# Ten of stage two's twelve units by seven block products, 13.6 filler products a run, and the third row pair's blocks loaded earlier in the queue

## The chip, the cores and the metric

The kernel runs on one core of one Trainium2 chip. The metric is the device time of one execution in microseconds (us), the median of the runs taken. Engines are named as in the profile: PE is TensorE's matmul, PEld its weight load, DVE is VectorE, ACT is ScalarE, POOL is GpSimd, SP is the engine that issues most transfers.

## What is computed

One layer (DEPTH is 1, so only mixer A runs) of an encoder over 2048 tokens of width 1024, 16 heads of 64, all in float32: a root-mean-square norm, one projection to queries, keys, values and a gate, 2-D neighbourhood attention on a 32 x 64 grid of tokens (8 x 16 neighbours, with a learned bias), a SiLU gate, the output projection, the residual and a last norm. Cut to what matters:

```python
h = rmsnorm(x, norm_0)
q, k, v, gate = split(h @ w_in_0, 4)
# per token: softmax over its 8 x 16 neighbours of q.k / 8 + bias, then the weighted sum of v
o = neighbourhood_attention(q, k, v, rpb_0)
x = x + (o * silu(gate)) @ w_out_0
return rmsnorm(x, norm_f)
```

## The kernel before

Float32 products are made of three matmuls on "fp32r" halves: each operand is split into a high part h (a copy on ACT) and a low part l (a subtraction on DVE), and h·h, h·l and l·h are added in PSUM. Nearly every matmul of the projections moves 512 columns against a 128 x 128 weight.

The program has four stages, written out by hand in one order for all engines; each engine then works off its own part of that order and waits only for data and buffers.

- **Stage one** (tokens 0 to 1023) and **stage two** (tokens 1024 to 2047) make the projections. A unit is 256 columns of q, k, v or g. `seven_products` computes a unit for 1024 tokens as a 2 x 2 block product with seven block products in place of eight (84 matmuls in place of 96); the sums of weight blocks (`sum_`), the splits (`form`) and the sums of results (`add`, `out_`) are extra work on DVE and ACT. In stage two `units_two` lists the units done so; before, nine of twelve: k, q and g of column groups 0, 1 and 2.
- **The attention stage** is a loop over m, 33 passes ("runs"). Run m makes the scores of one pair of heads and one tile of 512 tokens (`scores`: PE L1297; minimum and bias on DVE L1306; exponentials on ACT L1312), turns the weights of the pair before (`turns`: PE transposes `ph`, L1355; copies to `pta` on ACT L1345 and DVE L1343) and multiplies them with the values (`values`: PE `o`, L1374; the gate on DVE L1378). The order in it is: filler products, transposes of m-1, scores of m, values of m-1. Between the scores of m and their transposes lies one stretch of filler in run m+1: in it DVE takes a reciprocal of the sums (L1317), and POOL (L1324) and DVE (L1322) scale the weights (`normalise`). `feed(8)` puts eight filler products, with whatever copies, gates and splits fall due in them, ahead of that reciprocal in DVE's order; the rest of the filler comes behind it.
- **The filler** is, first, the projections that stage two left over (`projections`, plain products, 24 matmuls a group, PE L392 to L396; `halves` lists them; each group ends in `give`: for q and k a copy on ACT, for g a tanh on ACT L372 and a product on DVE L373), and then the output products of token tiles 0 to 5 (`outputs`, PE L1578 to L1582, 24 matmuls a group; each group ends in `add_rows`, a sum on DVE L1450). `split_og` splits a tile of the gated attention output into `gh` (ACT L1420) and `gl` (DVE L1421). `dense` is the number of filler products a run, and `amount` the list by run (alternately 1.5 more and less from run 8 to 23).
- **The last stage**, `rows_by_seven`, makes the output products of tiles 6 to 15 in five pairs, again seven block products a pair (PE `py`, L1670). `load_rows_of` (L1631) loads a block of a pair from the scratch `ogd`; `sum_rows` (L1643) adds blocks on DVE; `land` (L1602) brings the split blocks of the output weights. All of these transfers are issued by SP, in order. Buffers come from pools: `raw` has six, `qp` (the queries' pool) two.

Queries, keys, values and gates pass through scratch memory; each run loads those of the next.

Of the kernel before, what the change touches and what calls it, by code (L numbers as in the profile page):

```python
# [77 lines left out]
def build(ctx, tc, x, xr, xt, wg, bias, w_out, n0, nf, out):  # L78
# [22 lines left out]
    qp = pool("qp", 2)  # L101
# [155 lines left out]
    def units(k, j):  # L257
        return [KINDS[k] + j + i for i in range(2 if k == "v" else 1)]

    units_two = [(k, j) for j in range(3) for k in "kqg"]  # L260
    halves = [(k, 3, 1, c) for g in ("k", "qg") for c in (2, 3) for k in g]
    attending = [False]
    last_use = {}
    for n, (k, j, ph, c) in enumerate(halves):
# [5 lines left out]
    for n, (k, j, ph, c) in enumerate(halves):  # L270
        a = (KINDS[k] + j, ph)
# [66 lines left out]
    def store(key, lag, f):  # L338
        n = len(later)
        while n and later[n - 1][0] > clock[0] + lag:  # L340
            n -= 1
        later.insert(n, (clock[0] + lag, key, f))
# [853 lines left out]
    def projections():  # L1196
        for n, (kind, j, ph, c) in enumerate(halves):
            state["half"] = n
            w = (KINDS[kind] + j, ph)
            for a in range(2):  # L1200
                if n == len(halves) - 5 and a == 0:
                    for k in range(RES_EARLY):
                        load_res(*turns_[k])
                if n == len(halves) - 1:
                    if a == 0:
                        load_og(0)
                        load_og(1)
                    else:
                        store(("og0",), 9, lambda: split_og(0))
                consume(1)  # L1210
                p = yield from group(w, a, c, n)
                state["event"] = clock[0]
                give(kind, 2 * j + a, c, p, True)
            state["done_halves"] = n + 1
# [199 lines left out]
    def split_og(n):  # L1414
        t = G[n]
        state["event"] = clock[0]
        h, l = wp([128, NK, 128], F32R, "gh"), wp([128, NK, 128], F32R, "gl")
        for j in range(2):
            s = slice(4 * j, 4 * j + 4)
            nc.scalar.activation(h[:, s], t[:, s], AF.Copy)  # L1420
            nc.vector.tensor_tensor(l[:, s], t[:, s], h[:, s].bitcast(F32), OP.subtract)  # L1421
        G[n] = [(h[:, i], l[:, i]) for i in range(NK)]
# [176 lines left out]
    def land(where, homes):  # L1599
        for (f, k, i), h in zip(where, homes):  # L1600
            TF.setdefault(f, [[None, None] for _ in range(4)])[k][i] = h
            nc.sync.dma_start(h.bitcast(F32), wod[f][:, k, i])  # L1602
# [13 lines left out]
    def land_T2():  # L1616
        for f in ("A21", "A22"):
            load_rows_of(1, f, vh)
        for m in range(LEADERS):
            load_rest_of(m)  # L1620
        land([("T2", k, i) for k in range(4) for i in range(2)], [a[k, 1] for k in range(4) for a in (woh, wol)])

    def land_T4():
        land(parts7[17:], sixths() + [sp([128, 512], F32R, "t")])

    def load_rows_of(m, f, home=None):
        n, half = PAIRS[m][int(f[1]) - 1], int(f[2]) - 1
        T, i = divmod(n, 4)
        must(*[("og", p, T) for p in range(NP) if slot(T, p) // 4 == half])
        A[m, f] = (home or raw)([128, 512], F32, "raw")  # L1630
        nc.sync.dma_start(A[m, f].rearrange("p (k q) -> p k q", k=4), ogd[T][:, i, 4 * half:4 * half + 4])  # L1631
# [65 lines left out]
    def rows_by_seven():  # L1697
# [10 lines left out]
        def on(i, f, *a):  # L1708
            todo.setdefault(i, []).append((f, a))
# [4 lines left out]
            on(i, sum_rows, 1, f)  # L1714
        for i, f in ((8, "S1"), (9, "S2"), (10, "S3"), (12, "S4")):
            on(i, sum_rows, 2, f)
        for i, f in ((2, "A21"), (4, "A22")):
            on(i, load_rows_of, 2, f)
        for m in range(E, len(PAIRS)):
            s = seq.index((m, 6)) - 1  # L1720
            for d, f in ((-12, "A11"), (-10, "A21"), (-9, "A22"), (-7, "A12")) if m == E else \
# [18 lines left out]
                        f(*a)  # L1740

    cycles = len(order)
    dense, end_of_it = 16.5, 24
    amount = [dense] * 25
    first = 16
    amount[0] -= first / 2
# [56 lines left out]
    for m in range(cycles + 1):  # L1803
        a = amount[m] - 8
# [88 lines left out]
```

## Time and profile before

| what | us |
|---|---|
| median of 3 runs | 997.81 (997.7, 997.81, 1002.13) |
| the profiled execution, its own time | 1003.56 |
| its span, first to last instruction | 1001.5 |
| stage one, and the values of stage two, to about | 390 |
| stage two's nine units | 390 to 561 |
| attention stage | 561 to 895 |
| last stage | 895 to 1001.5 |

The span is 2 us shorter than the execution's own time. Rows of the timeline read: start, duration, engine, line and operation, count, and in brackets the idle time of the engine before the row and what ended it. Rows of the stretches read: the stretch, its length, busy time of PE, PEld, DVE, ACT and POOL with the number of instructions, the granted PE clock (1.00 is full), the share of the transfer engines, GB/s.

### The profile page before, as it was taken

The page shows a single profiled execution, that of the slowest core. Times are in us where ns is not written, and L with a number is a line of the kernel's source. Part 1 is how long each engine was busy: PE and PEld are TensorE (multiplying, and loading weights), DVE is VectorE, ACT ScalarE, POOL GpSimd, SP SyncE. Part 2 cuts the span into 40 slices and gives each one's busy share as a digit, 9 for nine tenths or more (in the row PEclk, how much of TensorE's full clock was granted, in tenths as well). Part 3 has the DMA queues.
Part 4 walks back from the last instruction along what each step waited for, and adds up shares of the span by engine and source line. Part 5 has one row for each costly group of instructions (what it writes and reads, how often), then busy time and mean ns, then how long its engine had stood idle before and what let it go on. Part 6 is the DMA issues. An engine that isn't in the chain of part 4 may idle for free.

```text
span 1001.5 us, 19560 instructions
## 1 busy us (share of the span) xinstructions
PE 991.0 (99%) x6904; PEld 793.1 (79%) x6904; DVE 772.4 (77%) x1704; ACT 520.4 (52%) x1271; POOL 149.5 (15%) x233
## 2 busy tenths in 40 slices
PE   9999999999999999999999999999999999999897
PEld 6888888888888888888888777777777777788786
DVE  5899888997666876766775677778888888885776
ACT  7873344454534433343434466667767666653443
POOL 0000001321100000000000123233333323212010
PEclk9999999999999999999999999999999999999999
DMA  8943547777957845655565798979887789799464
GB/s 288 340 128 96 196 142 252 240 245 256 348 162 224 259 134 182 220 185 184 200 205 179 220 281 244 277 239 287 286 252 255 207 263 286 243 335 319 132 187 116
DMA packets 149834, 227.67 MB, mean 227 GB/s; under 512 B 13608, under 2 KB 65064, under 8 KB 149736
## 3 DMA queue, kind: packets, MB, share of 16 engines
q1 hardware_dynamic: 147144, 222.09, 69.5%
q0 software_dynamic: 2160, 3.93, 2.4%
q8 instruction: 55, 0.90, 0.3%
q10 hardware_dynamic: 432, 0.40, 0.1%
q14 instruction: 43, 0.35, 0.1%
HBM read 160.31 MB, written 66.06 MB: 226 GB/s over the span
## 4 chain that ended last, share of the span: by engine, by line
PE 93%; DMA 4%; DVE 2%; ACT 1%; issue 0%; SPq 0%; DVEq 0%
PE pp L448 40%; PE pv L614 13%; PE o L1374 8%; PE s L1297 7%; PE py L1670 5%; PE ph L1355 4%; PE pp L394 2%; PE po L1578 2%; PE po L1580 2%; PE pp L396 2%; PE po L1582 2%; PE pp L392 2%; PE pv L729 2%; DMA raw<-ogd 1%; DMA ogd<-og 1%; DMA wol<-wodT 1%
## 5 line engine op out<-in xcount | busy, mean ns | idle before, releaser
L448 PE MATMUL pp<-h,f 128*128 128x512 f32 x576 | 185.4, 389 | 0.0
L1324 POOL TENSOR_SCALAR x<-x,st 128x360 f32<-128x360 f32 (+5 forms) x192 | 106.3, 570 | 521.5 <-DVE st L1317 520.2
L448 PE MATMUL pp<-t,f 128*128 128x512 f32 x702 | 171.6, 389 | 0.0
L448 PEld LDWEIGHTS pp<-t,f 128*128 128x128 f32 x702 | 131.6, 188 | 27.9 <-DVE u L461 0.4
L1312 ACT ACTIVATE x<-x,st 128x360 f32<-128x360 f32 (+5 forms) x256 | 134.1, 525 | 22.1 <-DVE st L1306 22.1
L448 PEld LDWEIGHTS pp<-h,f 128*128 128x128 f32 x576 | 108.1, 188 | 23.0 <-ACT p L456 0.5
L448 PE MATMUL pp<-l,f 128*128 128x512 f32 x288 | 112.1, 389 | 0.0
L1306 DVE CUSTOM_DVE_ANT_0 x<-s,em 128x360 f32<-128x360 f32 (+5 forms) x256 | 102.7, 456 | 3.6 <-PE s L1297 1.3
L431 DVE TENSOR_TENSOR f<-raw,f 128x512 fp32r<-128x512 f32 x105 | 75.9, 727 | 20.0 <-ACT f L430 19.8
L1374 PEld LDWEIGHTS o<-pta,vt 120*64 120x64 f32 (+2 forms) x1024 | 68.7, 137 | 22.4 <-DVE st L1306 15.2
L430 ACT ACTIVATE f<-raw 128x512 fp32r<-128x512 f32 x105 | 63.5, 622 | 38.6 <-DVE raw L437 22.0
L1374 PE MATMUL o<-pta,vt 120*64 120x192 f32 (+5 forms) x1024 | 83.5, 316 | 0.0
L1345 ACT ACTIVATE pta<-ph 120x512 f32<-120x512 f32 (+5 forms) x96 | 47.3, 557 | 59.4 <-PE ph L1355 59.4
L1343 DVE COPY pta<-ph 120x512 f32<-120x512 f32 (+5 forms) x96 | 56.1, 638 | 23.1 <-PE ph L1355 22.8
L1297 PE MATMUL s<-kt,q 64*64 64x360 f32 (+5 forms) x1024 | 71.3, 412 | 0.0
L448 PEld LDWEIGHTS pp<-l,f 128*128 128x128 f32 x288 | 54.1, 188 | 11.2
L614 PE MATMUL pv<-wh,t 128*128 128x512 f32 x176 | 56.2, 389 | 0.0
L1670 PE MATMUL py<-woh,f 128*128 128x512 f32 x160 | 52.2, 399 | 3.1 <-DVE y L1450 3.1
L448 PE MATMUL pp<-sixths,f 128*128 128x512 f32 x198 | 52.7, 389 | 0.0
L469 POOL TENSOR_TENSOR tmp<-tmp,rb 128x512 f32<-128x512 f32 x18 | 28.4, 1579 | 158.8 <-DVE tmp L466 128.0
L1297 PEld LDWEIGHTS s<-kt,q 64*64 64x64 f32 x1024 | 37.3, 132 | 18.6 <-ACT pta L1345 0.4
L1355 PEld LDWEIGHTS ph<-ident,x 64*120 64x120 f32 (+2 forms) x1408 | 42.5, 128 | 11.3 <-issue 9.2
(226 smaller groups left out, 1872.9 us busy)
## 6 DMA issues: line engine op xcount, KB each, us to landing
raw<-in_wg_dram SPq DMA_DIRECT2D x124, 256.0 KB, 5.0
row<-in_xr_dram SPq DMA_DIRECT2D x32, 256.0 KB, 5.2
vd<-v SPq DMA_DIRECT2D x32, 256.0 KB, 3.5
sgd<-sg SPq DMA_DIRECT2D x32, 256.0 KB, 5.1
q<-qd SPq DMA_DIRECT2D x32, 256.0 KB, 5.5
sgt<-sgd SPq DMA_DIRECT2D x32, 256.0 KB, 6.8
ogd<-og SPq DMA_DIRECT2D x32, 256.0 KB, 2.8
kt<-kd SPq DMA_DIRECT2D x16, 480.0 KB, 6.9
```

The lines of the kernel that those rows point to most:

```text
L430: nc.scalar.activation(t[:, 0], src, AF.Copy)
L431: nc.vector.tensor_tensor(t[:, 1], src, t[:, 0].bitcast(F32), OP.subtract)
L448: nc.tensor.matmul(B[n, P], t[:, int(m == 2), c], x[k][int(m == 1)], start=P in (1, 6, 5) and k == 0 and m == 0, stop=k == 3 and m == 2, s ...
L614: nc.tensor.matmul(p, a[:, o], b, start=P in (1, 6, 5) and k == 0 and m == 0, stop=k == 3 and m == 2, skip_group_check=True)
L1297: nc.tensor.matmul(places[C, s][h * 64:h * 64 + 64], qt[a, g * 64:g * 64 + 64], kt[a, :r1 - r0, c0:c0 + 8 * WIDE[C]].rearrange("p r (s c) ...
L1306: nc.vector.tensor_tensor_reduce(X[i, C][s], pst[s], EM[p, ROW_TYPE[T]][C > 0][s], -1.0, 1e38, OP.add, OP.min, st[:, o:o + 1])
L1312: nc.scalar.activation(X[i, C][s], X[i, C][s], AF.Exp, bias=st[:, o:o + 1], scale=-1.0, accum_out=st[:, 4 + o:5 + o])
L1324: nc.gpsimd.tensor_scalar(X[i, C][s], X[i, C][s], st[:, o:o + 1], 1.0, op0=OP.mult, op1=OP.mult)
L1343: nc.vector.tensor_copy(o, i_)
L1355: nc.tensor.transpose(ph[b, h][:k, o:o + 64], X[2 * m + late_, group[g]][s][q, at:at + k], ident[q, q])
L1374: nc.tensor.matmul(o[s * 64:s * 64 + 64, g0 * 64:g1 * 64], vt[:k, strip, s * 64:s * 64 + 64], t[:k, n * 64:(n + g1 - g0) * 64], start=stri ...
L1670: nc.tensor.matmul(B[m, P], t[:, a, c], b, start=P in (1, 6, 5) and k == 0 and i == 0, stop=k == 3 and i == 2, skip_group_check=True)
```

## The change

`units_two` gets a tenth unit, k of column group 3, and `halves` loses k's two halves: 84 matmuls come into stage two, and 96 leave the filler. `dense` goes from 16.5 to 13.6, so that the filler still lasts for all runs. The loads of the first residual block, of tiles 0 and 1 of the gated output, and the split of tile 0, which hang on positions in `halves`, are put at other positions. In the last stage the blocks A21 and A22 of the third pair (m = 2) are loaded at the end of `land_T2`, into the queries' pool, in place of at steps 2 and 4 of the sequence into `raw`.

```diff
-    units_two = [(k, j) for j in range(3) for k in "kqg"]
-    halves = [(k, 3, 1, c) for g in ("k", "qg") for c in (2, 3) for k in g]
+    units_two = [(k, j) for j in range(3) for k in "kqg"] + [("k", 3)]
+    halves = [(k, 3, 1, c) for c in (2, 3) for k in "qg"]
...
-                if n == len(halves) - 5 and a == 0:
+                if n == 0 and a == 1:
                     for k in range(RES_EARLY):
                         load_res(*turns_[k])
                 if n == len(halves) - 1:
-                    if a == 0:
+                    if a == 1:
                         load_og(0)
                         load_og(1)
-                    else:
-                        store(("og0",), 9, lambda: split_og(0))
+                        store(("og0",), 14, lambda: split_og(0))
...
         land([("T2", k, i) for k in range(4) for i in range(2)], [a[k, 1] for k in range(4) for a in (woh, wol)])
+        for f in ("A21", "A22"):
+            load_rows_of(2, f, qp)
...
-        for i, f in ((2, "A21"), (4, "A22")):
-            on(i, load_rows_of, 2, f)
...
-    dense, end_of_it = 16.5, 24
+    dense, end_of_it = 13.6, 24
```

The filler products that stand between two blocks of transposes on PE, counted in the order of the program (run m is the run in whose filler they stand):

| m | 2 | 3 | 4 | 5 | 11 | 12 | 13 | 17 | 19 | 21 | 26 | 27 | 28 |
|---|---|---|---|---|---|---|---|---|---|---|---|---|---|
| before | 18 | 15 | 16 | 17 | 15 | 21 | 12 | 15 | 15 | 15 | 16 | 17 | 19 |
| now | 10 | 14 | 13 | 14 | 12 | 16 | 12 | 12 | 12 | 9 | 13 | 13 | 13 |

Because the filler's groups now end at other places, other copies and splits fall ahead of the reciprocal. DVE in run 3, from the gate of the values (og) to the copies of the transposes, before:

```order
L1378 TENSOR_TENSOR og<-o,sgt 128x512
L1317 RECIPROCAL st<-st 128x4
L1322 TENSOR_SCALAR x_5999<-x_5999,st 128x264
L1322 TENSOR_SCALAR x_6000<-x_6000,st 128x264
L194 TENSOR_TENSOR w<-raw,w 128x512
L1343 COPY pta<-ph_6072 88x6x64
```

and now:

```order
L1377 TENSOR_TENSOR og<-o,sgt 128x512
L373 SCALAR_TENSOR_TENSOR sg<-sg,pp 128x512
L1316 RECIPROCAL st<-st 128x4
L1321 TENSOR_SCALAR x_5780<-x_5780,st 128x264
L1321 TENSOR_SCALAR x_5781<-x_5781,st 128x264
L542 SCALAR_TENSOR_TENSOR raw<-raw,g_174,rb 128x512
L547 TENSOR_TENSOR l<-raw,h 128x512
L1342 COPY pta<-ph_5852 88x6x64
```

A gate's product (sg) now stands ahead of the reciprocal, and a norm and a split of an input block (L542, L547) stand between the scaling and the copies. The filler group on which sg waits ends with the seventh product of this run.

DVE in run 26, before:

```order
L1378 TENSOR_TENSOR og<-o,sgt 128x512
L1450 TENSOR_TENSOR y<-po,xr 128x512
L1317 RECIPROCAL st<-st 128x4
L1322 TENSOR_SCALAR x_9702<-x_9702,st 128x288
L1322 TENSOR_SCALAR x_9703<-x_9703,st 128x288
L1492 SCALAR_TENSOR_TENSOR y<-y,st_8349,acc_175 128x512
L1492 SCALAR_TENSOR_TENSOR y<-y,st_8349,acc_176 128x512
L1421 TENSOR_TENSOR gl<-ograw,gh 128x512 x2
L1343 COPY pta<-ph_9780 96x6x64
```

and now:

```order
L1377 TENSOR_TENSOR og<-o,sgt 128x512
L1449 TENSOR_TENSOR y<-po,xr 128x512
L1420 TENSOR_TENSOR gl<-ograw,gh 128x512 x2
L1316 RECIPROCAL st<-st 128x4
L1321 TENSOR_SCALAR x_9750<-x_9750,st 128x288
L1321 TENSOR_SCALAR x_9751<-x_9751,st 128x288
L1420 TENSOR_TENSOR gl<-ograw,gh 128x512 x2
L1342 COPY pta<-ph_9830 96x6x64
```

The split of tile 4 has moved ahead of the reciprocal: the sixth filler product of this run is the first one that reads it, so it is made there and then. In the same way the split of tile 0 now stands ahead of the reciprocal in run 11.

SP at the start of the last stage, from the last of the T2 weights on, before:

```order
L1602 DMA wol<-wodT_95 128x512
L1602 DMA sixths<-wodT_97 128x512 x6
L1602 DMA t<-wodT_97 128x512
L1381 DMA ogd_88<-og 512x1x128
L1496 DMA out_dram<-y 128x512 x4
L1631 DMA raw<-ogd_87 128x512 x2
L1631 DMA raw<-ogd_88 128x512 x4
```

and now:

```order
L1601 DMA wol<-wodT_95 128x512
L1632 DMA raw<-ogd_87 128x512 x2
L1601 DMA sixths<-wodT_97 128x512 x6
L1601 DMA t<-wodT_97 128x512
L1380 DMA ogd_88<-og 512x1x128
L1495 DMA out_dram<-y 128x512 x2
L1632 DMA raw<-ogd_88 128x512 x4
```

The third pair's two blocks (from `ogd_87`) are now asked for ahead of the seven T4 weights, the last store of the attention output and the output rows.

## The prediction

> **What bounds the kernel now.** I read first the page's busy times and then what PE waited for.
>
> ```profile
> PE 991.0 (99%) x6904; PEld 793.1 (79%) x6904; DVE 772.4 (77%) x1704; ACT 520.4 (52%) x1271; POOL 149.5 (15%) x233
> PE py L1670 <- DVE y L1450: 3.1, 2, 2.8
> PE zp L135 <- DVE z L132: 1.2, 1, 1.2
> ```
>
> PE sets the end. In the whole span it waits in two places that count: at the start, and once in the last stage, 2.8 us on a sum of DVE. So a matmul saved is saved in full, if no new wait takes its place. The stretches show where one could:
>
> ```profile
> 390.00:561.00 171.00, 171.00 (x756) 141.65 (x755) 114.79 (x184) 62.83 (x112) 0.00 (x0) 1.00 0.61 198
> 658.00:893.00 235.00, 235.00 (x2855) 177.62 (x2853) 201.30 (x637) 160.07 (x493) 77.51 (x138) 1.00 0.85 264
> ```
>
> Stage two (first row) has DVE at 115 of 171 us, so another unit finds room there. In the attention stage (second row) DVE is busy 201 of 235 us, 86%, and PE is full only because the filler covers a chain of other engines. One run of that stage, from its block of transposes to the next one:
>
> ```profile
> 664.95 1.51 PE L1355 MATMUL ph<-ident,x 64*120 64x64 f32 x44
> 671.31 0.50 PE L394 MATMUL pp<-l,w 128*128 128x512 f32 x1
> 671.57 0.58 ACT L1312 ACTIVATE x<-x,st 128x360 f32<-128x360 f32 x1
> 672.28 0.18 DVE L1317 RECIPROCAL st<-st 128x4 f32<-128x4 f32 x1 [0.16 <-ACT x L1312]
> 672.62 1.34 POOL L1324 TENSOR_SCALAR x<-x,st 128x360 f32<-128x360 f32 x2 [0.32 <-DVE st L1317]
> 674.93 1.51 PE L1355 MATMUL ph<-ident,x 64*120 64x64 f32 x44
> ```
>
> This is run 11. The interval is 9.98 us with 15 filler products, which begin at 671.31. The chain runs over the last exponential (its accumulator is read by 672.2), the reciprocal and POOL's scaling, and is done at 673.96, 9.01 us after 664.95. PE came 0.97 us later, so it did not wait. Other runs have less to spare:
>
> ```profile
> 662.10 0.69 DVE L373 SCALAR_TENSOR_TENSOR sg<-sg,pp 128x512 f32<-128x512 f32 x1 [0.64 <-ACT sg L372]
> 662.70 0.17 DVE L1317 RECIPROCAL st<-st 128x4 f32<-128x4 f32 x1
> 663.07 1.83 POOL L1324 TENSOR_SCALAR x<-x,st 128x360 f32<-128x360 f32 x2 [1.42 <-DVE st L1317]
> 693.94 1.85 POOL L1324 TENSOR_SCALAR x<-x,st 128x360 f32<-128x360 f32 x2
> 695.73 1.51 PE L1355 MATMUL ph<-ident,x 64*120 64x64 f32 x44
> ```
>
> In run 10 a gate's product stands ahead of the reciprocal: the chain ends at 664.90, only 0.05 us before the transposes of 664.95. In run 13 (last two rows) POOL ended at 695.79, 0.06 us after the transposes had begun, and PE lost nothing: their first products read the weights scaled earlier. POOL's second piece is first read by the sixteenth of the 44 transposes; at 1.44 us for 44 that leaves 0.47 us of grace.
>
> **The matmuls.** 756 products took 171 us, 0.2262 each. 84 come, 96 go: 12 x 0.2262 = 2.7 us less. The tenth unit's sums and splits, 114.8 / 9 = 12.8 us of DVE in 19 us of PE, hide under its products; without that cover they would cost at most what exceeds 19 us, so nothing.
>
> **The third pair.** The one wait in the last stage:
>
> ```profile
> 906.50 4.30 SPq L1602 DMA_DIRECT2D sixths<-wodT  x6
> 916.02 0.41 SPq L1631 DMA_DIRECT2D raw<-ogd  x1
> 924.97 0.39 PE L1670 MATMUL py<-sixths,f 128*128 128x512 f32 x1
> 927.46 2.88 PE L1670 MATMUL py<-t,f 128*128 128x512 f32 x12
> 931.12 0.69 DVE L1643 TENSOR_TENSOR s<-raw 128x512 f32<-128x512 f32 x1 [10.93 <-DMA raw<-ogd]
> 932.33 0.69 DVE L1450 TENSOR_TENSOR y<-py,u 128x512 f32<-128x512 f32 x1
> 933.16 0.47 PE L1670 MATMUL py<-woh,f 128*128 128x512 f32 x1 [2.82 <-DVE y L1450]
> 933.00:937.50 4.50, 4.34 (x12) 3.47 (x13) 4.50 (x9) 2.66 (x7) 0.00 (x0) 0.62 0.19 57
> 937.57 0.40 PE L1670 MATMUL py<-t,f 128*128 128x512 f32 x1
> 954.30 0.47 PE L1670 MATMUL py<-woh,f 128*128 128x512 f32 x1 [0.24 <-DVE y L1450]
> ```
>
> DVE stands 10.93 us before a sum of the third pair, whose blocks SP asked for at 916.02; the sum that frees PE's bank (932.33) is queued behind it. PE's last product before the gap started at about 929.95, the next could have started at 930.18 and did so at 933.16: 3.0 us. Then the granted clock is 0.62 over the stretch (1.00 elsewhere), and the 12 products from 933.16 to 937.57 took 4.41 us in place of 2.72: 1.7 us. Together 4.7 us. With the change SP asks for the blocks where it asked for the T4 weights, at 906.5, ten us sooner, and DVE wants them at 920.2 (931.12 less 10.93). Their buffers in the queries' pool were last read by scores of run 31, long over. The T4 weights move two issues back, about 1.4 us by the spacing of this row (4.30 for six); PE first reads them at 924.97, more than 13 us after their issue, so this hides; if it did not, the same pair would wait that 1.4 us. For the profiled execution I take the full 4.7 us.
>
> The median run is 997.81, the profiled one 1003.56, and one of the three timed runs is 4.3 us above the two others. That is close to the size of this stall, the largest on PE, so it may be smaller in the median run. Its gain there lies between 0 and 4.7 us; I take 3.5, nearer to the one execution that shows it.
>
> **The attention stage.** Fewer filler products make each interval shorter by 0.2268 a product. For runs like run 11 the interval by products alone is 9.98 - 15 x 0.2268 = 6.58 us plus 0.2268 a product. With 12 products it is 9.30 and the undisturbed chain (9.01, less 0.47 of grace) still fits; with 9 (run 21) it is 8.62 against 8.54 to 9.0 (POOL's pair takes 1.34 to 1.83). So the plain runs cost nothing or little: 0.3 us for runs 19 and 21. The cost is in the runs where something new stands ahead of the reciprocal. Tokens' tile 0 first, rows of run 2, whose shape run 3 shares:
>
> ```profile
> 576.32 1.43 PE L1355 MATMUL ph<-ident,x 64*88 64x64 f32 x44
> 582.01 0.50 PE L394 MATMUL pp<-l,w 128*128 128x512 f32 x1
> 583.15 0.18 DVE L1317 RECIPROCAL st<-st 128x4 f32<-128x4 f32 x1 [0.33 <-ACT x L1312]
> 583.50 1.59 POOL L1324 TENSOR_SCALAR x<-x,st 128x264 f32<-128x264 f32 x2 [0.27 <-DVE st L1317]
> 586.33 1.43 PE L1355 MATMUL ph<-ident,x 64*88 64x64 f32 x44
> ```
>
> The interval is 10.01 with 18 products, so 5.93 plus 0.2268 a product; run 3 will have 14: 9.1 us. Its gate's group ends with the seventh product, which starts 1.5 us after the first and takes 0.4: 7.6 us from the block. Tanh 0.6, sg 0.7, reciprocal and hand-over 0.3 (as in run 10), POOL 1.59: 10.8, less the grace 10.3. PE waits 1.2. In runs 2 to 4 the split of an input block (L542 0.7, a copy on ACT 0.6, L547 0.7) stands between the scaling and the copies of the transposes, and ACT's copy ahead of ACT's. What that costs shows where ACT's copies came 0.6 late:
>
> ```profile
> 840.71 0.63 ACT L1453 ACTIVATE xr<-y 128x512 f32<-128x512 f32 x1 [2.17 <-DVE y L1450]
> 841.34 1.43 ACT L1345 ACTIVATE pta<-ph 96x384 f32<-96x384 f32 x3
> 831.56 1.94 PE s L1297 x32
> 841.52 2.34 PE s L1297 x32
> ```
>
> The scores behind them (last row) took 0.4 us longer than those of the run before. I take 0.4 for run 3 and 0.6 for run 4: with the above 2.2 us for runs 2 to 4. Run 5 has sg too, its group ending with the fourth product: 9.4 against 9.1, 0.3 us.
>
> Run 11 (split of tile 0 ahead of the reciprocal): exponentials done at 7.2 us, two copies 0.6 each, the second subtraction ends at 9.1, reciprocal and POOL 1.5: 10.6, less 0.47, against 9.30: 0.9 us. Run 13, whose copies on DVE start about 1 us late behind run 12's splits: 0.3 us. Run 17, a sum that waits for the fifth product: 0.4 us, by these rows of run 30, where it waited for the sixth:
>
> ```profile
> 860.15 1.43 PE L1355 MATMUL ph<-ident,x 64*96 64x64 f32 x44
> 867.00 0.19 ACT L1312 ACTIVATION_READ_ACCUMULATOR x<-x,st 128x1 f32 x1
> 867.70 0.69 DVE L1450 TENSOR_TENSOR y<-po,xr 128x512 f32<-128x512 f32 x1 [0.90 <-PE po L1582]
> 868.64 1.14 POOL L1324 TENSOR_SCALAR x<-x,st 128x288 f32<-128x288 f32 x2 [1.36 <-DVE st L1317]
> ```
>
> There the sum moved the reciprocal about 1 us past the last accumulator. Run 26 is the dearest. Its block stands where run 30's did at 860.15; the sum ends at 7.95 us, the first subtraction of tile 4's low part at 8.6, and PE's second product on that tile needs it: seven more products end at 10.4 against 9.05 (run 30 took 9.73 with 16, so 6.10 plus 13 x 0.2268). 1.4 us. The sum of these is 2.2 + 0.3 + 0.9 + 0.3 + 0.4 + 0.3 + 1.4 = 5.8; the runs before lose 0.4 at 841.52 and 0.4 on a weight's split, and those places go: 5.0 us net.
>
> ```profile
> PEld po L1582 <- DVE wol L199: 0.4, 1, 0.4
> ```
>
> Bounds: 0, if the splits fall where PE still has products; 10, if no grace exists (0.47 us more in about ten runs). I take 5.0.
>
> **Sum.** For the profiled execution -2.7 - 4.7 + 5.0 = -2.4 us on 1003.56. For the median -2.7 - 3.5 + 5.0 = -1.2: 996.6 us. The other edits (the residual block and the tiles asked for at other products) only change places in SP's queue ahead of readers a run away, and cost nothing; uncovered, a late tile would cost a few us in run 11 alone.
>
> **The rivals.** Half a per cent, 5.0 us, is about what a measurement can tell from no change.
>
> Faster: the waits do not come, because ACT and DVE reach their work early in shorter runs; the cost of the stage stays under 2 us and the stall goes in full: -2.7 - 4.7 + 1.5 = -5.9, 991.9 us. For it speaks run 13 above, against it that sg and gl are ahead of the reciprocal by order.
>
> The earlier load brings nothing in the median run, because the stall is a matter of the profiled execution: -2.7 + 5.0 = 2.3, 1000.1 us. For it speaks the gap of 5.8 us between the median and the profiled run, against it that the stall is caused by the order of SP's queue.
>
> Slower: the clock. A gap of 3.2 us between two products' starts halved it and cost 1.7 us more; 0.6 us (954.30) did not. If 1 us is enough, runs 3, 4, 11 and 26 each pay 1.7 us on top of their wait: -1.2 + 6.8 = 5.6, 1003.4 us. It decides from two such runs on with the third pair's gain lost, from four with it. The Trainium skill, page "TensorE: Matmul & The Clock Gate", section "What's actually happening", says that the clock falls back after an idle window of about 3.4 us; the trace shows it after less (2.82 idle), so the page's bound is not kept here, but by it none of these waits could halve the clock, and this rival would fall away with the forecast unchanged at 996.6.
>
> **How the numbers follow.** Forecast 0.35 (996.6, its own range 994 to 999), no gain from the load 0.25, faster 0.27, the clock or waits above 10 us 0.13. The first two are within half a per cent. The range: from 991.0, all gains with 0.6 us of waits, to 1002.0, no gain from the load and waits of 7. Chances: faster 0.27, same 0.60, slower 0.13.
>
> **What would show it.** Stage two's stretch grows to 190 us with DVE at two thirds. In the third pair DVE no longer waits for `raw<-ogd` and the granted clock in the last stage is 1.00: if a wait of several us is left there, that term is wrong. In the attention stage run 26 shows PE waiting for gl, runs 3 and 11 show transposes waiting for POOL by about 1 us; if PE has no gaps above 0.5 us between 560 and 880, the 5.0 us are wrong. If the granted clock falls below 1.00 there, the clock rival holds.

## The result, and the profile after

The change made the kernel slower by about half a per cent: 1004.1 us (median of 5, 1003.79 to 1004.93) against 998.03 (median of 5, 997.7 to 1002.13) for the kernel before; the ratio is 1.0049, with a 95% interval of 1.0028 to 1.0070. The forecast was 996.6, with a range up to 1002.0, so both its size and its direction were wrong.

The profile after has a span of 1002.7 us, only 1.2 more than the 1001.5 of the profile before. That comparison misleads, as the first experiment shows. First the busy times of the page and what PE waited for (total, times, longest), then three stretches in the columns used before: stage two, the attention stage from run 2 on, the last stage.

```profile
PE 991.1 (99%) x6892; PEld 792.9 (79%) x6892; DVE 778.8 (78%) x1716; ACT 522.3 (52%) x1272; POOL 149.5 (15%) x233
PE ph L1354 <- POOL x L1323: 2.8, 8, 0.7
PE zp L135 <- DVE z L132: 1.2, 1, 1.2
PE po L1579 <- DVE gl L1420: 0.5, 1, 0.5
PE po L1577 <- ACT gh L1419: 0.3, 1, 0.3
390.00:580.00 190.00, 190.00 (x840) 157.40 (x840) 126.56 (x201) 70.04 (x124) 0.00 (x0) 1.00 0.58 190
597.00:897.00 300.00, 295.78 (x3711) 220.57 (x3705) 255.03 (x839) 205.62 (x646) 103.50 (x186) 1.00 0.86 266
901.00:1002.60 101.60, 95.61 (x420) 78.59 (x420) 75.12 (x147) 42.30 (x99) 13.26 (x15) 0.98 0.71 205
```

Stage two is as forecast: 190 us, DVE at two thirds. The last stage is 5 us shorter than in the profile before; its clock is 1.00 up to 999.4 and lower only in the last 3 us, when PE has finished, as in the kernel before. The wait of `py` on DVE's sum is gone from the list; in its place stand waits of `ph` on POOL and of `po` on tile 4's split. They sum to 3.6 us, but such a list leaves out transposes and scores that run slowly because PE's weight loads wait. A fuller measure is the **loss** of a run: the time from its first transpose to the next run's, less the length by products alone that the prediction used (5.93, 6.58 or 6.10 us plus 0.2268 a product; 6.52 and 6.51 in the two runs where the tile's width changes). Summed over runs 2 to 32 it is 0.97 us before and 10.75 after. A wait in run r's transposes or scores counts in interval r+1; the table puts it back to run r. Its first row is the exception: it holds intervals 2 to 4, which begin with the transposes and scores of runs 1 to 3, the runs with input blocks to split.

| place | forecast | measured |
|---|---|---|
| runs 2 to 4 | 2.2 | 0.53 + 0.81 + 1.62 = 2.96 |
| run 5 | 0.3 | 0.63 |
| run 11 | 0.9 | 1.40 |
| runs 12 and 13 | 0.3 | 0.93 |
| run 17 | 0.4 | 1.00 |
| runs 19 to 21 | 0.3 | 0.22 + 0.56 = 0.78 |
| run 23 | 0 | 0.92 |
| runs 26 and 27 | 1.4 | 1.68 |
| others | 0 | 0.4 |
| gone from before | -0.8 | -0.97 |
| net | 5.0 | 9.8 |

Every row that the forecast named does wait; its size is too small in each of them, and run 23 was missed. Split by what PE was doing, the 10.75 us are 5.8 in the transposes (3.1 forecast), 3.5 in the scores behind them (1.3) and 1.4 in the filler of run 26 (1.4). Four places show why. Run 3 and the start of run 4's transposes, in rows of the timeline, sorted by time:

```profile
611.60 0.69 DVE L373 SCALAR_TENSOR_TENSOR sg<-sg,pp 128x512 f32<-128x512 f32 x1 [1.42 <-ACT sg L372]
612.20 0.17 DVE L1316 RECIPROCAL st<-st 128x4 f32<-128x4 f32 x1
612.46 0.53 PE L1354 MATMUL ph<-ident,x 64*88 64x64 f32 x11
612.57 1.05 POOL L1323 TENSOR_SCALAR x<-x,st 128x264 f32<-128x264 f32 x2 [1.76 <-DVE st L1316]
613.17 0.31 PE L1354 MATMUL ph<-ident,x 64*88 64x64 f32 x4 [0.18 <-POOL x L1323]
613.19 0.96 DVE L542 SCALAR_TENSOR_TENSOR raw<-raw,g,rb 128x512 f32<-128x512 f32 x1
613.67 1.03 PE L1354 MATMUL ph<-ident,x 64*88 64x64 f32 x29 [0.18 <-POOL x L1323]
614.63 2.69 PE L1296 MATMUL s<-kt,q 64*64 64x176 f32 x32
614.85 0.69 DVE L547 TENSOR_TENSOR l<-raw,h 128x512 fp32r<-128x512 f32 x1 [0.70 <-ACT h L546]
615.46 1.74 DVE L1342 COPY pta<-ph 88x384 f32<-88x384 f32 x3
621.82 1.07 POOL L1323 TENSOR_SCALAR x<-x,st 128x264 f32<-128x264 f32 x2 [0.27 <-DVE st L1316]
622.96 1.43 PE L1354 MATMUL ph<-ident,x 64*88 64x64 f32 x44
624.32 1.86 PE L1296 MATMUL s<-kt,q 64*64 64x176 f32 x32
```

The gate's product is there ahead of the reciprocal, as forecast, and PE waits for POOL twice: from the first transpose to the first score it takes 2.17 us, against 1.36 in the next block (622.96 to 624.32). That is 0.81 us where 1.2 was forecast. The other part comes behind: the norm and the split of an input block hold DVE until 615.46, so its copies of the transposes start 3.0 us after the transposes (612.46). The scores wait for these copies: they take 2.69 us, against 1.86 in the next block, so 0.83 more. The two together are the whole loss of this interval, 1.62; its values and its filler take no longer than by products alone, and POOL is done with run 4's weights at 622.89, 0.07 us ahead of their transposes. The forecast gave such a split 0.4 to 0.6 us, from a row in which ACT's copies came 0.6 us late. The scores of run 2, with the same two works ahead of the copies, lose 0.81 as well, and those of run 1 0.36.

Run 21 (the first two rows) and run 23, DVE, POOL and PE:

```profile
789.42 1.70 DVE L1491 SCALAR_TENSOR_TENSOR y<-y,st,acc 128x512 f32<-128x512 f32 x2
788.59 1.33 POOL L1323 TENSOR_SCALAR x<-x,st 128x360 f32<-128x360 f32 x2 [0.32 <-DVE st L1316]
807.96 0.73 DVE L1321 TENSOR_SCALAR x<-x,st 128x360 f32<-128x360 f32 x2
808.60 1.64 DVE L1491 SCALAR_TENSOR_TENSOR y<-y,st,acc 128x512 f32<-128x512 f32 x2
808.38 2.29 POOL L1323 TENSOR_SCALAR x<-x,st 128x360 f32<-128x360 f32 x2 [0.61 <-DVE x L1321]
809.43 0.68 PE L1354 MATMUL ph<-ident,x 64*120 64x64 f32 x15
810.72 1.10 PE L1354 MATMUL ph<-ident,x 64*120 64x64 f32 x29 [0.61 <-POOL x L1323]
```

Nothing stands ahead of these reciprocals. In both runs DVE goes on to scale rows of the output. In run 21 POOL is ahead of it, its pair takes 1.33 us and DVE's 1.70; only the copies behind are late, and the scores lose 0.53. In run 23 POOL starts 0.3 us later, behind DVE's own scaling (0.61 in its bracket against 0.32), DVE's products come between, and POOL's pair takes 2.29. The sixteenth transpose waits for it, as the forecast's 0.47 us of grace had it, and the block loses 0.88.

Run 17 has a row sum ahead of the reciprocal, as forecast, and then a split of weights on DVE beside POOL:

```profile
749.22 1.85 POOL L1323 TENSOR_SCALAR x<-x,st 128x360 f32<-128x360 f32 x2 [1.41 <-DVE st L1316]
```

This pair takes 0.5 us more than in run 21, and run 17 loses 0.6 more than was forecast.

Run 26, where the forecast was right:

```profile
836.52 2.18 ACT L1419 ACTIVATE gh<-ograw 128x512 fp32r<-128x512 f32 x4
837.49 1.28 DVE L1420 TENSOR_TENSOR gl<-ograw,gh 128x512 fp32r<-128x512 f32 x2
837.19 0.50 PE L1577 MATMUL po<-woh,gh 128*128 128x512 f32 x1 [0.35 <-ACT gh L1419]
838.23 0.50 PE L1579 MATMUL po<-woh,gl 128*128 128x512 f32 x1 [0.54 <-DVE gl L1420]
```

PE has come to tile 4's rows before they are split, and waits first for the high part and then for the low part, 1.40 us in all.

### The profile page after: what moved, and what is told of

It is laid out like the page before. It is cut to its first block, busy times and chain, and to the rows that moved or that the text cites. A ratio compares the mean times of both kernels' runs of the same rounds, so it can differ in the third digit from the quotient of the medians.

```text
span 1002.7 us, 19545 instructions
## 1 busy us (share of the span) xinstructions
PE 991.1 (99%) x6892; PEld 792.9 (79%) x6892; DVE 778.8 (78%) x1716; ACT 522.3 (52%) x1272; POOL 149.5 (15%) x233
## 4 chain that ended last, share of the span: by engine, by line
PE 92%; DMA 3%; ACT 1%; DVE 1%; POOL 1%; issue 0%; SPq 0%; POOLq 0%; DVEq 0%
PE pp L448 42%; PE pv L614 13%; PE py L1671 10%; PE o L1373 7%; PE s L1296 6%; PE ph L1354 4%; PE pv L729 2%; PE po L1579 2%; PE po L1577 2%; PE po L1581 2%; POOL x L1323 1%; PE pp L394 1%; PE pp L396 1%; PE pp L392 1%; DMA ograw<-ogd 1%; ACT x L1311 1%
## 5 line engine op out<-in xcount | busy, mean ns | idle before, releaser
L448 PE MATMUL pp<-h,f 128*128 128x512 f32 x608 | 195.8, 389 | 0.0
L448 PE MATMUL pp<-t,f 128*128 128x512 f32 x728 | 178.1, 389 | 0.0
L448 PEld LDWEIGHTS pp<-t,f 128*128 128x128 f32 x728 | 136.7, 188 | 28.3
L448 PEld LDWEIGHTS pp<-h,f 128*128 128x128 f32 x608 | 114.2, 188 | 23.7
L448 PE MATMUL pp<-l,f 128*128 128x512 f32 x304 | 118.4, 389 | 0.0
L431 DVE TENSOR_TENSOR f<-raw,f 128x512 fp32r<-128x512 f32 x110 | 79.2, 725 | 19.9 <-ACT f L430 19.8
L430 ACT ACTIVATE f<-raw 128x512 fp32r<-128x512 f32 x110 | 66.5, 622 | 39.1 <-DVE raw L437 22.2
L448 PEld LDWEIGHTS pp<-l,f 128*128 128x128 f32 x304 | 57.1, 188 | 11.9
L430 ACT ACTIVATE f<-s 128x512 fp32r<-128x512 f32 x44 | 27.5, 624 | 49.4 <-DVE s L437 40.8
L1354 PE MATMUL ph<-ident,x 64*120 64x64 f32 (+2 forms) x1408 | 49.4, 221 | 2.9 <-POOL x L1323 2.8
```

What stands on the lines that cost most here:

```text
L430: nc.scalar.activation(t[:, 0], src, AF.Copy)
L431: nc.vector.tensor_tensor(t[:, 1], src, t[:, 0].bitcast(F32), OP.subtract)
L448: nc.tensor.matmul(B[n, P], t[:, int(m == 2), c], x[k][int(m == 1)], start=P in (1, 6, 5) and k == 0 and m == 0, stop=k == 3 and m == 2, s ...
L1354: nc.tensor.transpose(ph[b, h][:k, o:o + 64], X[2 * m + late_, group[g]][s][q, at:at + k], ident[q, q])
```

## The experiments

All loss figures are of the one profiled execution of each kernel, all ratios against the kernel before in the same set of runs.

| run | median us | ratio to before (95%) | loss of the attention stage |
|---|---|---|---|
| the changed kernel | 1004.10 | 1.0049 (1.0028 to 1.0070) | 10.75 |
| c0 | 998.11 | 0.9996 (0.9978 to 1.0013) | 0.9 |
| e1 | 997.94 | 0.9993 (0.9979 to 1.0007) | 0.9 |
| e2 | 1005.20 | 1.0062 (1.0039 to 1.0086) | 10.6 |
| e3 | 1003.54 | 1.0043 (1.0028 to 1.0058) | 6.4 |
| e4 | 1005.81 | 1.0068 (1.0052 to 1.0084) | 10.9 |
| e5 | 1003.00 | 1.0045 (1.0029 to 1.0060) | 9.5 |
| e6 | 1006.13 | 1.0075 (1.0060 to 1.0090) | 8.8 |
| e10 | 1004.38 | 1.0063 (1.0050 to 1.0075) | 9.6 |
| e11 | 1012.37 | 1.0147 (1.0133 to 1.0161) | 19.0 |
| e12 | 1008.10 | 1.0102 (1.0086 to 1.0117) | 14.2 |
| e13 | 1001.42 | 1.0020 (1.0004 to 1.0036) | 7.7 |
| e14 | 1002.44 | 1.0038 (1.0020 to 1.0056) | 5.6 |
| e15 | 1002.37 | 1.0048 (1.0030 to 1.0066) | 3.4 |
| e16 | 1011.82 | 1.0133 (1.0117 to 1.0149) | 17.2 |
| e17 | 1002.78 | 1.0039 (1.0027 to 1.0051) | 7.0 |
| e18 | 1002.65 | 1.0038 (1.0024 to 1.0053) | 8.6 |

### The third pair: c0, e1 and e2

c0 is the kernel before again.

> The kernel before, unchanged, to see whether its profiled execution shows the third pair's stall again and which of its executions have it. Theory 1 (the stall is an event of some executions): the profile either has it (span near 1001.5, clock 0.997) or has not (span near 996, no wait of the py products above 1 us), and the executions fall into two groups about 4 to 5 us apart, 997.8 and 1002 to 1003.5, of which the larger is the faster one. Theory 2 (the stall is in every execution and the profiled one is slower for another reason): every profile shows the gap of 2.8 to 3.0 us and the times stay within 1 us.

e1 is the kernel before with the blocks sooner, and nothing else:

```diff
         land([("T2", k, i) for k in range(4) for i in range(2)], [a[k, 1] for k in range(4) for a in (woh, wol)])
+        for f in ("A21", "A22"):
+            load_rows_of(2, f, qp)
...
-        for i, f in ((2, "A21"), (4, "A22")):
-            on(i, load_rows_of, 2, f)
```

> The kernel before with the third pair's two blocks asked for sooner, and nothing else. Theory 1 (the stall is in few executions): median 997.5 to 998.2, that is no gain against the median of before, but no execution above 1000 and a profiled span near 996.5, against 1001.5 of before. Theory 2 (the stall is in all executions): 993.3 to 994.5, that is 3.5 to 4.7 us faster.

e2 is the changed kernel with the same lines undone.

> The changed kernel with the third pair's two blocks asked for where the kernel before asks for them. Theory 1 (in before the stall is in few executions): about 1004 in most executions, and 1008 in those that have the stall. Theory 2 (the earlier request gains 3.5 to 4.7 us in all executions, and the attention stage costs about 12): 1007.6 to 1008.8. A third possibility: with one product of time less ahead of it the stall comes more often than in before, and the median lies between.

c0's profile has a span of 995.7 us and no wait of `py`. Its rows in the place where the profile before has its stall, SP first, then DVE:

```profile
904.79 3.48 SPq L1602 DMA_DIRECT2D sixths<-wodT  x6
913.00 4.19 SPq L1631 DMA_DIRECT2D raw<-ogd  x4
925.24 0.69 DVE L1643 TENSOR_TENSOR s<-raw 128x512 f32<-128x512 f32 x1 [5.62 <-DMA raw<-ogd]
926.45 0.69 DVE L1450 TENSOR_TENSOR y<-py,u 128x512 f32<-128x512 f32 x1
894.10:995.60 101.50, 95.51 (x422) 78.75 (x420) 75.70 (x149) 42.02 (x99) 13.26 (x15) 0.99 0.70 206
```

DVE waits here too, 5.62 us for the same block, but the sum that frees PE's bank still comes in time. In the profile before SP was 3.0 us later with the block (916.02), the transfer itself took 15.1 us until DVE could start where here it took 12.2, and DVE waited 10.93. So the stall is the same order plus a late transfer, and most executions can't have it in full: of c0's ten, seven lie between 997.6 and 998.3 and three above 1000, the highest 1003.35. That those three had this stall is not shown, since none of them was profiled, and the times don't fall into two groups as theory 1 had it: of the 29 executions of the kernel before in the same set, 14 lie below 998.6, twelve from there to 1001.2 and three above. e1 confirms from the other side that the median has no such stall: its ratio of 0.9993 is a gain of 0.7 us, by the interval at most 2.1, though in its profile DVE no longer waits for the block; its highest execution is 1000.44 where before reaches 1004.26. e2's profile shows `py` waiting 1.1 us for the sum and 1.0 for a split, and two of its six executions lie above 1007; its median can't be told from the changed kernel's. The theory that the stall belongs to single executions holds in the main, the other falls: the earlier request is worth about 5 us in an execution like the profiled one, and 0.7, not to be told from nothing, in the median.

With c0 the account closes: from its span to that of the changed kernel it is 7.0 us, and -2.7 for twelve matmuls plus 9.8 of new loss is 7.1. Timed it is 6.1.

### Thin filler alone: e3 and e14

```diff
-    dense, end_of_it = 16.5, 24
+    dense, end_of_it = 13.6, 24
```

on the kernel before, with its nine units (e3), and the same with 15.0 (e14).

> The kernel before with 13.6 products of filler a run in place of 16.5 in the first 25 runs, nine units in stage two, the same number of matmuls; the filler saved goes to the last seven runs, 26.9 each. Theory 1 (the thin filler is what costs): the runs up to 24 lose about 7 to 8 us against products alone, as in the changed kernel, the waits on tile low parts in runs 26 and 27 are gone, median 1005 to 1006. Rival (the loss comes from what the changed list of units moves: the input blocks and weights split in runs 2 to 4 and 12, or stage two): under 3 us lost, median below 1001.

> The kernel before with 15.0 products of filler a run in place of 16.5 in the first 25 runs, nine units, the rest in the last seven runs (21.9 each). e3 with 13.6 lost 6.4 us in the profile where before loses 0.9. Theory 1 (a run costs nothing until its own slack is used up; in before POOL is done 0.35 to 2.8 us ahead of need, 22 of 31 runs with over 1 us): 1.5 products are 0.34 us a run, so the loss stays below 2.5 us, 997.5 to 999.5. Rival (every product taken from a run costs in proportion, because DVE is full): half of e3's loss, 3.7 us or more, 1000.5 to 1001.5.

What PE waited for, e3's row first, then e14's:

```profile
PE ph L1355 <- POOL x L1324: 2.8, 5, 0.8
```

```profile
PE ph L1355 <- POOL x L1324: 2.2, 6, 0.8
```

e3 loses 5.5 us more than before with the same matmuls and no change in stage two, and is 1.0043 times as slow: over half of the changed kernel's loss comes with the filler alone. Its median lies below the range expected, since runs 2 to 6, which cost the changed kernel 3.6 us, lose 0.2: before's list of halves has no input block left to split there. e14 goes against theory 1, which had the loss below 2.5 with slack by run, and its 5.6 us are not in proportion to the products taken either, which would be 3.7; its time is above both ranges. It loses nearly what e3 does, 4.0 us of it in runs 9, 11, 16 and 17, where DVE has a gate or a split of a tile ahead of the reciprocal; in before only run 10 has one there.

### Order alone: e4, e6, e5

e4 (on the changed kernel) and e6 (on the kernel before) put the reciprocal first in DVE's order:

```diff
-        a = amount[m] - 8
+        a = amount[m] - 1
...
-        feed(8)
+        feed(1)
```

> The changed kernel with one product of filler in place of eight ahead of the reciprocal in the program, so that DVE's order has the reciprocal and the scaling ahead of the run's gate (sg), split (gl) or row sum (y). Theory 1 (those works ahead of the reciprocal cost the waits of runs 3, 5, 11, 17 and 26, 0.8 + 0.6 + 1.4 + 1.0 + 1.4 = 5.2 us of the 10.7): they go, the same works behind the scaling cost up to 1 us in runs 3, 13 and 26, where they delay the copies of the transposes: 999 to 1001.5. Rival (DVE is simply too busy in a thin run, and the order does not matter): the waits move from POOL's scaling to DVE's copies, loss still 9 to 11 us, 1003 to 1005.

> The kernel before with one product of filler in place of eight ahead of the reciprocal in the program. It loses 0.9 us against products alone, so both theories let it gain at most that: 997 to 998.2. Above 999 it would show that the order by itself brings new waits.

PE's waits in e4, then in e6:

```profile
PE s L1296 <- ACT pta L1344: 2.5, 2, 2.1
PE po L1579 <- DVE gl L1420: 0.7, 1, 0.7
PE ph L1354 <- POOL x L1323: 0.6, 1, 0.6
```

```profile
PE s L1297 <- DVE y L1450: 2.4, 1, 2.4
PE s L1297 <- ACT pta L1345: 2.1, 2, 1.6
```

The rival holds for e4: the waits on POOL fall from 2.8 to 0.6 us, and those of the scores on the copies come instead. The loss stays, and the time is just above the rival's range. e6 is a miss for both theories, which gave it no loss, and its sign of new waits, a time above 999, holds: even with 16.5 products the order costs 8 us, 6.2 of it in one place, run 26, where nine works (rows of the output, two tiles' splits and a row sum) now stand between the scaling and the copies. The eight products ahead of the reciprocal have their use: what falls there would else stand behind it.

e5 takes one input from the products beside POOL. It leaves out the factor of each column in those rows, so it serves for the timing alone:

```diff
-                    nc.vector.scalar_tensor_tensor(y[j], y[j], r, late["nf"][j], op0=OP.mult, op1=OP.mult)
+                    nc.vector.tensor_scalar(y[j], y[j], r, None, op0=OP.mult)
```

> The changed kernel with the final scaling of the six plain tiles' rows made with one tensor as input (y times its row's factor) in place of two (the factor of each column is left out of those rows). Theory 1 (POOL's scaling of the probabilities is stretched while DVE reads two tensors): in run 23, where the pair on POOL took 2.29 us beside two such products, it takes 1.3 to 1.5, its transposes do not wait, and the loss of the interval behind it, 0.9 us, goes; 1003 to 1003.6 in all. Rival (POOL is slow there for having started behind the scaling on DVE, whatever runs beside it): the pair stays above 2 us and the loss stays.

Run 23 in e5:

```profile
807.80 1.11 DVE L1491 TENSOR_SCALAR y<-y,st 128x512 f32<-128x512 f32 x2
807.58 1.76 POOL L1323 TENSOR_SCALAR x<-x,st 128x360 f32<-128x360 f32 x2 [0.61 <-DVE x L1321]
808.63 1.86 PE L1354 MATMUL ph<-ident,x 64*120 64x64 f32 x44
```

POOL's pair takes 1.76 us, 0.53 less than with two inputs, and the block of transposes loses 0.35 us in place of 0.88. The pair does not fall to 1.3 to 1.5 as theory 1 had it, so beside products with one tensor it is still 0.4 longer than in run 21; that DVE's pair is shorter (1.11 against 1.64) may be part of the gain. The loss of the stage falls by 1.2 us, 0.5 of it in run 23 and 0.5 in run 21.

### More filler where runs wait: e10, e11, e12, e13

e10 takes the alternation away (`+= 0`). e11, e12 and e13 add to the list of amounts by run. This is e11's list; those of e12 and e13 are longer and also take products from other runs:

```diff
+    for m, more in ((2, 2.5), (3, 6), (4, 2), (5, 3.5)):
+        amount[m] += more
```

> The changed kernel without the alternation of 1.5 products more and less between even and odd runs; the order of DVE's work stays nearly the same. Theory 1 (each waiting run lacks filler for its own chain): the odd runs 11, 17 and 23 get 1.5 products more and lose about 0.34 us less each, the even runs keep slack: loss 9 to 10 us in place of 10.7, 1002.5 to 1003.6. Rival (the alternation matches work that stands in even runs): new waits in even runs, 1004.5 or more.

> The changed kernel with 2.5, 6, 2 and 3.5 products more in runs 2 to 5, and 2 fewer in each of the last seven. Theory 1 (the runs whose gate and input splits stand in the chain lack filler): the loss of intervals 2 to 6, 3.6 us now, falls below 1.2, and the last seven runs have the slack (POOL there is done 0.6 to 2.5 us ahead of need): 1001 to 1002.5. Rival (the copies of the transposes are late behind the splits on DVE, however long the run): the loss of intervals 4 and 6 stays, 1003.5 to 1004.5.

> The changed kernel with a table of products by run: more where the changed kernel waits (runs 2 to 5, 11, 12, 17, 21, 23: 31.5 products), less where POOL is done 1 us or more ahead of need (runs 8, 10, 14, 18, 20, 22, 24: 21 products), the rest from the last seven runs. Theory 1 (slack and waits are local to a run): loss 3 to 6 us, 997.5 to 1000.5. Rival (filler that moves takes the gates, splits and row sums with it, and new waits come where these land): loss 8 us or more, 1002 to 1005.

> The changed kernel with a second table of products by run: 33 more in runs 2 to 5, 11, 12, 15, 17, 21 and 23, 34 fewer in runs 6 to 10, 14, 18 to 20, 22 and 24, so that up to run 24 it is 1.5 fewer than in the changed kernel and tile 4's rows are not wanted before they are there, which cost e12 some 8 us in one place. Theory 1 (waits and slack are local): no wait above 2 us, loss of the attention stage 4 to 7 us, 998.5 to 1001. Rival (filler that moves only moves the waits, for its gates, splits and row sums land ahead of other reciprocals): loss 8 us or more, 1002 or more.

e10 can't be told from the changed kernel: its loss of 9.6 lies in theory 1's range, its time above it, and what run 11 gains (0.8) runs 12 and 17 lose again. e11 and e12 are misses by 8 to 10 us for their first theory, yet their runs 2 to 6 lose 0.8 us where the changed kernel loses 3.6: that theory was right in its place. What costs is another place, here in e12:

```profile
831.86 1.15 ACT L1419 ACTIVATE gh<-ograw 128x512 fp32r<-128x512 f32 x2 [8.18 <-DMA ograw<-ogd]
832.54 0.79 PE L1577 MATMUL po<-woh,gh 128*128 128x512 f32 x1 [7.84 <-ACT gh L1419]
824.00:840.00 16.00, 8.16 (x102) 5.50 (x102) 6.70 (x20) 4.45 (x12) 1.14 (x2) 0.79 0.77 237
```

The products added up to run 24 (10.5 in e12, 14 in e11) bring PE to tile 4 one run sooner, in run 25, and tile 4's rows are attention results that have only just been stored: SP issues a store at 823.23 and asks for the rows at 825.61. PE stands for 7.84 us, and the granted clock over these 16 us is 0.79. e13, whose list is 1.5 products below the changed kernel's up to run 24, has no such wait: it loses 7.7 us, just over its range of 4 to 7, and at 1001.42 it is the fastest kernel with ten units, but still 1.0020 times before (the interval excludes 1).

### What a wait needs: e15, e16, e17, e18

```diff
-    dense, end_of_it = 16.5, 24
+    dense, end_of_it = 17.5, 24
```

on the kernel before is e15; e16 is the changed kernel with 14.0 in place of 13.6.

> The kernel before with 17.5 products of filler a run in place of 16.5 in the first 25 runs, nine units (the last seven runs get 12.9 each). Theory A (less filler means waits): every run up to 24 has 0.23 us more, the last seven have 0.8 us less, of which most have 1 to 2.6 us to spare: loss 1 to 2 us, 997.5 to 999. Theory B (16.5 is a count at which the gates, splits and row sums happen to land behind the reciprocals, and any other count deals them anew): a split of two halves now stands ahead of the reciprocal in runs 14 and 26; waits of 0.7 us or more there, loss 3.5 to 6 us, 1000.5 to 1003, although the runs are longer.

> The changed kernel with 14.0 products a run in place of 13.6 in the first 25 runs (the last seven get 11.7). Theory A: 0.09 us a run more, so waits change by under 1.5 us in all, the same runs wait: 1002.5 to 1004.5. Theory B: the order is another (gates ahead of the reciprocal in runs 11 and 13 and no longer in 3 and 5, tile 0's split in run 12, tile 4's behind), so the waits of runs 2 to 6, 3.6 us, go but for 0.6, new ones come in 11 to 13, and tile 4's 1.4 us shrink; by a sum over such places 2 to 3 us better: 1001 to 1002.5.

e15's attention stage loses 3.4 us, just below theory B's range, and its time of 1002.37 lies in it. But the split ahead of run 14's reciprocal costs nothing there, with 22 products in the run; the loss is in runs 17, 20 and 26, and in the dearest place (run 26's filler, 1.5 us) PE comes to a tile's rows before they are split, as in the changed kernel. Its executions spread from 999.89 to 1007.49, and the profiled one is the lowest, so this loss is not that of the median, whose further 2 us stay unexplained. More filler is no gain either. e16 is a miss for both: its order is not the one expected, since the gates of runs 3 and 5 are still ahead of the reciprocal, and 0.4 products a run are enough to bring tile 4 forward as in e12, for 8.3 us in one wait.

Over the profiles up to here, one for each order of the attention stage, so twelve (c0, e1 and two others repeat an order), runs 2 to 24, counted afterwards: of 30 runs with a gate or a tile's split ahead of the reciprocal, POOL was late for the sixteenth transpose in 21 of 21 with 15 products or fewer, and in 2 of 9 with more. Of 215 runs with neither (nor a row sum) ahead, it was late in 15 of 77 with 13 products or fewer and in 1 of 138 with more. e17 and e18 are ten-unit kernels with thin runs and nothing ahead:

```diff
-    dense, end_of_it = 13.6, 24
+    dense, end_of_it = 13.0, 24
...
-        amount[m] += 1.5 if m % 2 == 0 else -1.5
+        amount[m] += 1 if m % 2 == 0 else -1
+    for m, more in ((2, 2.5), (3, 6), (4, 1), (5, 3), (6, -1), (7, -2), (8, -2)):
+        amount[m] += more
...
-        a = amount[m] - 8
+        a = amount[m] - 4
...
-        feed(8)
+        feed(4)
```

> The changed kernel with amounts chosen so that no gate and no split stands ahead of the reciprocal in any run (4 products ahead of it in place of 8; 13.0 a run, alternating by 1; 2.5, 6, 1 and 3 more in runs 2 to 5, 1, 2 and 2 fewer in runs 6 to 8). Theory C (a wait needs both, a gate or split ahead of the reciprocal and a run of 15 products or fewer; without the first, a thin run mostly keeps time): the attention stage loses 3 to 6 us, of it 1.4 at tile 4, and the time is 998 to 1001. Rival (as in e4, what no longer stands ahead of the reciprocal makes the copies late by as much): loss 8 us or more, 1002 to 1005.

> The changed kernel with 5 products ahead of the reciprocal in place of 8 and 13.2 in every one of the first 25 runs, without the alternation and without more in the first runs; again no gate and no split stands ahead of a reciprocal. Theory C: as e17, but run 3 has an input's split and a gate behind each other ahead of its copies, which in e4 cost 2.9 us: loss 6 to 8 us, 1000.5 to 1002.5. Rival (late copies cost as much as a late scaling): loss 9 us or more, 1003 or more.

In both, POOL is in time for the sixteenth transpose in all 32 runs. So without a gate or a split ahead a thin run mostly keeps its scaling in time, though not always: the 15 of 77 above, run 23 of the changed kernel among them, were late without one. But e17 still loses 7.0 us, more than theory C said, and e18 8.6; both times lie above theory C's ranges. Run 21 of e17 shows where, and the last two rows are what PE and PE's weights waited for:

```profile
782.92 0.69 DVE L1449 TENSOR_TENSOR y<-po,xr 128x512 f32<-128x512 f32 x1
783.53 1.74 DVE L1342 COPY pta<-ph 120x384 f32<-120x384 f32 x3
783.66 3.65 PE L1296 MATMUL s<-kt,q 64*64 64x240 f32 x32
PE s L1296 <- DMA kt<-kd: 2.2, 2, 1.7
PEld s L1296 <- DVE pta L1342: 3.0, 5, 1.8
```

The row sum, now behind the scaling and the small steps of a root, holds the copies, and the scores behind them take 3.65 us, where 2.45 is the rule for this shape; run 23 loses the same 1.2 us there. And a run's keys come 1.7 us late, in e18 too. So the rival has a share too: part of the wait moved to the copies. Of the kernels run, none beats the kernel before by more than a measurement can tell; e1 equals it in the median, with fewer late executions.

## Why the prediction was wrong

**The matmuls, stage two, the clock.** Right as far as can be seen: 190 us for 840 products, and the account above closes with -2.7. The granted clock was 1.00 through the attention stage with waits of up to 1.04 us between two products' starts, so the clock rival is out.

**The third pair.** The step that failed is "I take 3.5, nearer to the one execution that shows it". The mechanism was right: in the changed kernel DVE has no wait on the block, and the last stage is 5 us shorter than in the profile before. But the profiled execution was the exception: the median run doesn't have the stall (c0, e1), and the term of 3.5 measured 0.7, by e1's interval between -0.7 and 2.1. The warning stood in the numbers: the profiled execution took 1003.56 and two of three timed ones 997.7 and 997.81. A stall that makes up most of that difference can't also be in the median. The rival "the earlier load brings nothing in the median" had this right, and its own sum with the measured loss, -2.7 + 9.8, gives 1004.9 for 997.81.

**The attention stage.** The term of 5.0 measured 9.8, with three parts mis-sized. First, "I take 0.4 for run 3 and 0.6 for run 4", the price of work between the scaling and the copies. It was read from a place where ACT's copies came 0.6 us late and the scores lost 0.4; here DVE's copies start up to 3 us after the transposes, and the scores of runs 1, 2 and 3 lose 0.36, 0.81 and 0.83. Run 12 belongs here too, 0.93 where 0.3 was forecast: 0.48 in the scores, and 0.44 in the transposes, behind a gate ahead of its reciprocal that the forecast had not counted. Second, the rows of the output that DVE scales behind the reciprocal were given nothing: POOL's pair beside them takes 2.29 us where it was taken at 1.34 to 1.83 (run 23, 0.92), and they hold the copies (run 21, 0.56); e5, with shorter ones, recovers 1.0 in these two runs. Third, runs 5, 11 and 17 lose 3.0 us where 1.6 was forecast; the mechanism is the one named, each chain is some tenths longer, in run 17 by the 0.5 of POOL's pair. Against these stands run 3's wait for POOL, 0.81 where 1.2 was forecast. Run 26 came out as forecast but for 0.3 us in its transposes. That the bound of 10 was nearly reached is no accident of one place: 15.0 and 13.6 products on nine units lose 4.6 and 5.5 us more than 16.5 in their profiles, and 17.5 loses 2.5 more. The order of the kernel before fits its 16.5 products; each other count that was tried deals gates, splits and row sums to other runs.

## What to carry to other kernels

Before a stall of a profile goes into a sum against a median, see whether the profiled execution's own time is that of the median; where it is longer by about the stall, the stall is worth little there. Filler that hides a chain of other engines is worth more than its own time: after a change of its amount, list for each run what stands ahead of the chain's first step and how many products the run has, since most waits had both, and price work that stands between the chain and the copies by the scores that wait for these copies. Moving filler to where a run waits also moves what it consumes forward, and that can hit data that are not there yet.

## What the runs showed of the hardware

POOL and DVE hold each other up, and the start goes with who pays: in run 21, where POOL's pair starts 0.83 us ahead of two products of DVE, it takes 1.33 us and they take 1.70; in run 23, where it starts 0.22 us ahead of them, it takes 2.29 and they 1.64. With no scaling of POOL beside them such products take 1.41 (c0's last stage). The Trainium skill, page "GPSIMD Engine Reference", section "1. Specifications", says that POOL shares its interfaces to SBUF with VectorE and contends with instructions that have two SBUF inputs or run in a two-port mode. The trace agrees that there is such a loss, by up to 0.96 us a pair.

PE's clock kept 1.00 in the changed kernel's attention stage, with gaps of up to 1.04 us between two products' starts, and fell within the wait of 7.84 us in e12 (0.78 over the wait, 0.77 over the 7.5 us behind it).

The transfer of the third pair's block took 12.2 us in one execution and 15.1 in another of the same program, from SP's request until DVE could start; that difference, on top of a request 3.0 us later, separates the stalled execution from the other.
